# The modulation vectors of a hybrid diffusion block: products with w_mod on TensorE's four column groups in place of multiply-adds on VectorE, ScalarE and GpSimd

## The chip, the core and the metric

The kernel runs on one core of one Trainium2 chip. A core has five engines with a queue each: TensorE (PE in the profile, its weight loads PEld), VectorE (DVE), ScalarE (ACT), GpSimd (POOL) and SyncE (SP), which here issues all DMAs. The metric is the device time of one execution in microseconds (us).

## The reference, cut to what matters

Two layers (`DEPTH = 2`) run over 1024 latent tokens and 256 context tokens of width `D = 1024`. Ahead of each layer six modulation vectors are made for the latent stream (from `c`) and six for the context stream (from `c_ctx`): a product of a row of 1024 numbers with a 1024 x 6144 matrix, in float32.

```python
sc_x = jax.nn.silu(c)
sc_c = jax.nn.silu(c_ctx)
for l in range(DEPTH):
    with_ctx = l < DEPTH - 1
    mod_x = (sc_x @ w_mod[l] + b_mod[l])[:, None, :]
    mod_c = sc_c @ w_mod[l] + b_mod[l]
    sh1_x, s1_x, g1_x, sh2_x, s2_x, g2_x = jnp.split(mod_x, 6, -1)
    sh1_c, s1_c, g1_c, sh2_c, s2_c, g2_c = jnp.split(mod_c, 6, -1)
    hx = rmsnorm(x, g_pre_mix[l]) * (1 + s1_x) + sh1_x
    px = hx @ w_in[l]
    yx, yc = hybrid_mix(px, pc, ...)          # conv, retention, Fourier, neighbourhood attention
    x = x + g1_x * rmsnorm(yx @ w_out[l], g_post_mix[l])
    hx = rmsnorm(x, g_pre_ffn[l]) * (1 + s2_x) + sh2_x
    x = x + g2_x * rmsnorm(conv_ffn(hx, w_up[l], ffn_conv_w[l], w_down[l]), g_post_ffn[l])
    ...                                        # the same for ctx where with_ctx
```

## The kernel before

All large products run on TensorE as three float32r products each (high by high, high by low, low by high: lines 311 to 313, 335 to 337, 1069 to 1071, 1207 to 1209). The tokens lie in tiles of 128, eight of the latent stream and two of the context (numbers 8 and 9).

A layer runs in this order. `fnet` does the Fourier mixing (lines 409 to 455; in layer 0 also for the context, lines 436 to 448). `retention` goes over ten token tiles three times, with three sets of projected columns: values (evacuated by `ev_v`, line 498), keys (`ev_k`, with `rotate` at line 520 and products at line 542), and queries with gates (`ev_qg`, whose first ScalarE step is line 573). Neighbourhood attention, the convolution, the output projection and the gated MLP follow. In the MLP a group of two blocks of 128 hidden columns is projected up (`up`), and `down` takes it through eight token tiles, adding each result to `acc` on VectorE (line 1287).

The modulation is spread over this work by a Python generator. `mod_pool` does a little with each `next`. Layer 0 takes the first third of its columns (`t = 0`) from a routine of its own, `mod_front` (line 923, products of the 128 x 32 tile `sc` with 256 columns, in four column groups), ahead of all else; the other two thirds come from `it`, which advances by two at four places of each half of `fnet` and after each token tile of `retention` (`step(2)`). All of layer 1's modulation comes from `it2`, which advances in layer 0's MLP, once or twice after each tile of `down` (line 1288), and is run out in `ctx_h2` (line 1170). What is done at each step before: a 128 x 512 tile of `w_mod` has come by DMA, and it is multiplied by one column of `sc_c` and added to an accumulator, for the latent stream on VectorE (line 210), for the context in layer 0 by a product on ScalarE (line 207) and an addition on GpSimd (line 208). After eight such tiles `sums` adds the accumulator over partitions on TensorE, a float32 product of 512 columns with a 32-column tile of zeros and one column of ones (line 182), into the j-th 32 partitions of a PSUM bank `X`. After four of them the bank is copied (line 185), transposed (line 218), and added to the bias (line 224); for the gates two small DMAs of 4-byte elements write `grow` (line 246).

Each pool tag has a fixed number of buffers, and a DMA into one is issued once its last readers are done; SP issues in order, so what stands behind such a DMA waits too. The order of the instructions on each engine is set by a scheduler at build time, which keeps near the order of the program; TensorE and the other engines work their queues in order.

Of the kernel before, what the change touches and what calls it, by code (L numbers as in the profile page):

```python
# [8 lines left out]
AF = mybir.ActivationFunctionType  # L9
ALU = mybir.AluOpType  # L10
# [4 lines left out]
P = 128  # L15
# [5 lines left out]
KT = 8  # L21
# [7 lines left out]
def build(tc, d, out, dbg=None):  # L29
    nc = tc.nc  # L30
    act, dve, pool, pe, sp = nc.scalar, nc.vector, nc.gpsimd, nc.tensor, nc.sync
# [20 lines left out]
    cst = Pool("cst", bufs=1, side="left")  # L52
    lay = Pool("lay", bufs=2, side="left")
    hp_ = Pool("h", bufs=1, side="left")
# [26 lines left out]
    def X():  # L81
        return cur["pool"].t([P, 512], "X", cur["tags"]["X"])
# [10 lines left out]
    sc_c = cst.t([P, KT, 2], "sc_c")  # L93
    sp.dma_start(out=sc_c, in_=d["cc"])
    act.activation(sc_c, sc_c, AF.Silu)
    hot = cst.t([P, 33], "hot")
    dve.memset(hot, 0.0)
    dve.memset(hot[:, 1:2], 1.0)
    late = {}

    def late_consts():
# [53 lines left out]
        act.activation(m.cd, m.cd, AF.Exp)  # L155
        act.activation(m.cd, m.cd, AF.Exp, scale=-128.0)

    def mod_pool(m, ts, both, acc_tile, w_tile, ahead, tmp_tile=None):

        l = m.l
        work = [(t, j, k) for t in ts for j in range(4) for k in range(KT)]
        ws = {}

        def load(i):
            if i < len(work):
                t, j, k = work[i]
                w = ws[i] = w_tile(i)
                c0 = 2048 * t + 512 * j  # L170
                sp.dma_start(out=w, in_=d["w_mod"][l, P * k : P * k + P, c0 : c0 + 512])

        for i in range(ahead):
            load(i)
        later = []
        prs = {}

        def sums(t, j, acc, ns):
            if j == 0:
                prs[t] = X()  # L180
            for s in range(ns):
                pe.matmul(prs[t][32 * j : 32 * j + 32, :], hot[:, 1 - s : 33 - s], acc[:, s], start=(s == 0), stop=(s == ns - 1))
            if j == 3:
                mr = acc_tile()[:, 0]
                act.copy(mr, prs.pop(t))
                later.append((i + 2, lambda: mod_out(m, t, mr)))

        for i in range(len(work) + 8):
            if later and (i >= later[0][0] or i >= len(work)):
                later.pop(0)[1]()  # L190
            if i >= len(work):
                if not later:
                    return
                yield
                continue
            t, j, k = work[i]
            if k == 0:
                acc = acc_tile()
            load(i + ahead)
            w = ws.pop(i)  # L200
            ns = 1 + both(t)
            for s in range(ns):
                if k == 0:
                    act.activation(acc[:, s], w, AF.Copy, scale=sc_c[:, k, s : s + 1])
                elif s and tmp_tile:
                    p = tmp_tile()
                    act.activation(p, w, AF.Copy, scale=sc_c[:, k, s : s + 1])
                    pool.tensor_add(acc[:, s], acc[:, s], p)
                else:
                    dve.scalar_tensor_tensor(acc[:, s], w, sc_c[:, k, s : s + 1], acc[:, s], ALU.mult, ALU.add)  # L210
            if k == KT - 1:
                later.append((i + 8, lambda t=t, j=j, acc=acc, ns=ns: sums(t, j, acc, ns)))
            yield

    def mod_out(m, t, mr):
# [627 lines left out]
    m = mod_cols(0)  # L843
# [36 lines left out]
    for l in range(DEPTH):  # L880
        with_ctx = l < DEPTH - 1
        m = mods[l]
# [5 lines left out]
        if l == 0:  # L888
            xs = {t: (d["x"][P * t : P * t + P] if t < NT else d["ctx"][P * (t - NT) : P * (t - NT) + P]) for t in tiles}
            nm = Pool("nm0", bufs=1, side="left")  # L890
            hh, hl = h_tiles()
            ch, cl = hc_tiles()
            tok = Tok(hh, hl, ch, cl)
            sc = nm.t([P, KT, 32], "sc")
            dve.memset(sc, 0.0)
            dve.tensor_copy(sc[:, :, 0:2], sc_c)
            par1 = nm.t([P, KT], "par1")
            dve.tensor_scalar_add(par1, m.par[:, 8:16], 1.0)
            wm, xn = {}, {}

            def load_wm(k):
                if k < KT:
                    wm[k] = nm.t([P, KT, 256], "wm", 2)
                    sp.dma_start(out=wm[k], in_=d["w_modf"][k])

            def norm_in(t):
                x = xn[t] = nm.t([P, D], "xn", 10)
                sp.dma_start(out=x, in_=xs[t])
                ss = sm.t([P, 1], "ss")
                act.activation(raw_tile(), x, AF.Square, accum_out=ss)  # L910
                r = rstd_of(ss)
                dve.tensor_scalar_mul(x, x, r[:, 0:1])

            def mod_front(k):

                if k == KT:
                    return
                load_wm(k + 1)
                pr = X()
                w = wm.pop(k)  # L920
                for kk in range(KT):
                    j = kk % 4
                    pe.matmul(pr[32 * j : 32 * j + 32, 0:256], sc[:, kk, :], w[:, kk, :], start=(kk < 4), stop=(kk >= 4))
                mr = nm.t([P, 256], "mr", 2)
                act.copy(mr, pr[:, 0:256])
                for b in range(2):
                    pe.transpose(pr[:, 256 + P * b : 384 + P * b], mr[:, P * b : P * b + P], ident)
                red = sm.t([P, 2, 2], "red")
                dve.reduce_sum(red, pr[:, 256:512].rearrange("p (b j s) -> p b s j", b=2, j=4)[:, :, 0:2], axis=AX)
                dve.tensor_scalar(m.mc[:, 0, k], red[:, 0], m.par[:, k : k + 1], None, ALU.add)  # L930
                dve.tensor_scalar(m.a1[:, k], red[:, 1], par1[:, k : k + 1], m.par[:, 48 + k : 49 + k], ALU.add, ALU.mult)

            def lat_k(k):
                if k < KT:
                    for n0 in (0, 4):
                        ns = slice(P * n0, P * n0 + 512)
                        to_hk(k, [xn[t] for t in range(n0, n0 + 4)], hh[k][:, ns], hl[k][:, ns], m.a1, m.mc[:, 0], 0,
                              nm.t([P, 512], "tmp", 3), G())

            def ctx_k(k):  # L940
                to_hk(k, [xn[8], xn[9]], ch[:, k, :], cl[:, k, :], m.a1, m.mc[:, 0], 1, nm.t([P, 512], "tmp", 3), G())

            load_wm(0)
            for t in range(4):
                norm_in(t)
            ws = [weight(wi[0]), weight(wi[1])]
            for t in range(4, 8):
                norm_in(t)
            mod_front(0)
            lat_k(0)  # L950
            for t in (8, 9):
                norm_in(t)
            mod_front(1)
            late_consts()
            mod_small(m)
            pin = [M2(), M2()]
            for k in range(KT):
                lat_k(k + 1)
                if k + 2 <= KT:
                    mod_front(k + 2)  # L960
                for mm in range(2):
                    for ci, c in enumerate(LAT):
                        project(tok, ws[mm], c, pin[mm][:, 512 * ci : 512 * ci + 512], [k])
                ctx_k(k)
            nm.close()
        else:
            xs = nf.xs
            tok = Tok(nf.hh, nf.hl)
            ws = [weight(wi[0]), weight(wi[1])]
            pin = [M2(), M2()]  # L970
            for mm in range(2):
                for ci, c in enumerate(LAT):
                    project(tok, ws[mm], c, pin[mm][:, 512 * ci : 512 * ci + 512])
            tok.ch, tok.cl = nf.ctx([nf.load(t) for t in (8, 9)])
            nf.pool.close()


        if l == 0:
            it = mod_pool(m, (1, 2), lambda t: 1, lambda: mw.t([P, 2, 512], "ma", 2), lambda i: mw.t([P, 512], "mw", 4), 3,
                          lambda: mw.t([P, 512], "mp", 2))  # L980
        else:
            it = iter(())

# [6 lines left out]
        mw = Pool(f"mw{l}", bufs=1, side="right")  # L990
# [9 lines left out]
        kk = nat_k(tok, wi[13], kp, rest)  # L1000
# [8 lines left out]
        for hp in range(2):  # L1009
            if hp:  # L1010
                kk = nat_k(tok, wi[15], kp)
# [134 lines left out]
        if l + 1 < DEPTH:  # L1146
            m2 = mods[l + 1] = mod_cols(l + 1)
            mod_small(m2)

            mp = {}  # L1150

            def acc2():
                mp[0] = hp_.t([P, 4, 512], "HC", 2)
                return mp[0][:, 0:2]

            def w2(i):
                return mp[0][:, 2 + i % 2]

            it2 = mod_pool(m2, (0, 1, 2), lambda t: t == 0, acc2, w2, 0)
        else:  # L1160
            it2 = iter(())
        mxs = [0]
# [298 lines left out]
```

## Time and profile before

| | |
|---|---|
| time, median of 3 runs | 2867.41 us (2867.34 to 2869.33) |
| profiled execution: time | 2867.49 us |
| profiled execution: span of the trace | 2865.6 us |
| busy PE / PEld | 2763.4 us (96%) / 2277.0 us (79%) |
| busy DVE / ACT / POOL | 1634.7 us (57%) / 1079.2 us (38%) / 216.4 us (8%) |
| chain of work that ended last | PE 78%, DVE 4%, ACT 1%, DMA 1% |
| DMA | 271.30 MB, mean 95 GB/s |

The busy time of an engine is the time in which it runs an instruction; of TensorE the end of a product is modelled, and products overlap, so that two starts in a row tell what one costs and the length of one does not. The granted clock (PEclk) is the share of full speed that TensorE was given. The chain of work follows what released each instruction back from the end; a share of PE of 78% says that in most of the span TensorE waits for nobody.

### The profile page before, as it was taken

The numbers are of one execution on the slowest core, as the hardware profiler recorded it, in microseconds if no ns is written. First come the engines' busy times: TensorE is split into PE (matmuls) and PEld (weight loads), VectorE is DVE, ScalarE is ACT, GpSimd is POOL, SyncE is SP. The second block draws the span as 40 slices with busy tenths as digits, with TensorE's granted clock in tenths as the row PEclk, the third lists the DMA queues.
The fourth block names the chain that finished last, engine by engine and source line by source line (L and its number), as shares of the span: only waits on it lengthen the run. The fifth ranks groups of instructions, "written<-read, shape, count | busy, mean of one in ns | idle before, by whom it ended". The sixth has DMA issues, their size and how long they took to land.

```text
span 2865.6 us, 36418 instructions
## 1 busy us (share of the span) xinstructions
PE 2763.4 (96%) x14368; PEld 2277.0 (79%) x14368; DVE 1634.7 (57%) x2629; ACT 1079.2 (38%) x1785; POOL 216.4 (8%) x214
## 2 busy tenths in 40 slices
PE   7879999999999999989999999999999999999998
PEld 4767788887888788878779988788878888888886
DVE  5974464647456555555697855555553444444455
ACT  4542353535433333222356632354444322323331
POOL 0643100010000000000030000200000000000002
PEclk9989999999999999999999999999999999999999
DMA  6531312353222232242376531222521111111113
GB/s 247 195 103 33 79 39 69 108 168 119 66 74 81 74 103 81 70 107 74 87 259 220 176 101 30 62 62 64 179 95 43 57 47 52 46 51 52 44 46 124
DMA packets 142739, 271.30 MB, mean 95 GB/s; under 512 B 46948, under 2 KB 71015, under 8 KB 141543
## 3 DMA queue, kind: packets, MB, share of 16 engines
q1 hardware_dynamic: 142566, 268.96, 29.8%
q8 instruction: 113, 1.85, 0.3%
q14 instruction: 60, 0.48, 0.1%
HBM read 235.59 MB, written 28.34 MB: 92 GB/s over the span
## 4 chain that ended last, share of the span: by engine, by line
PE 78%; DVE 4%; ACT 1%; DMA 1%; issue 1%; POOL 1%; DVEq 0%; POOLq 0%; ACTq 0%; SPq 0%
PE G L312 15%; PE G L311 15%; PE G L313 15%; PE M L1207 6%; PE M L1208 5%; PE M L1209 5%; PE M L1071 2%; PE M L1070 2%; PE M L1069 2%; PE T L793 1%; PE G L335 1%; PE G L337 1%; PE G L336 1%; PE T L778 1%; DVE acc L1287 1%
## 5 line engine op out<-in xcount | busy, mean ns | idle before, releaser
L311 PE MATMUL G<-H,WH 128*128 128x512 f32 x1792 | 701.7, 392 | 9.6 <-DVE nkl L697 6.0
L312 PE MATMUL G<-H,WH 128*128 128x512 f32 x1792 | 700.4, 391 | 0.2
L313 PE MATMUL G<-H,WL 128*128 128x512 f32 x1792 | 700.2, 391 | 0.0
L117 DVE TENSOR_TENSOR WL<-RAW,WH 128x1024 fp32r<-128x1024 f32 x242 | 294.6, 1224 | 510.8 <-ACT WH L116 510.1
L116 ACT CAST WH<-RAW 128x1024 fp32r<-128x1024 f32 x242 | 252.3, 1051 | 587.7 <-PE G L312 379.9
L311 PEld LDWEIGHTS G<-H,WH 128*128 128x128 f32 x1792 | 336.6, 188 | 81.2 <-issue 12.3
L312 PEld LDWEIGHTS G<-H,WH 128*128 128x128 f32 x1792 | 336.5, 188 | 69.1 <-DVE H L274 1.2
L313 PEld LDWEIGHTS G<-H,WL 128*128 128x128 f32 x1792 | 336.5, 188 | 67.8 <-issue 0.5
L1207 PE MATMUL M<-WH,gh 128*128 128x512 f32 x744 | 296.2, 398 | 11.1 <-DVE acc L1287 10.4
L1208 PE MATMUL M<-WL,gh 128*128 128x512 f32 x744 | 294.2, 395 | 2.7 <-DVE WL L117 2.7
L1209 PE MATMUL M<-WH,gl 128*128 128x512 f32 x744 | 292.8, 394 | 0.0
L1287 DVE TENSOR_TENSOR acc<-M,acc 128x1024 f32<-128x1024 f32 x151 | 184.3, 1220 | 81.1 <-PE M L1209 79.4
L1207 PEld LDWEIGHTS M<-WH,gh 128*128 128x128 f32 x744 | 141.5, 190 | 48.7 <-DVE acc L1287 13.7
L1191 ACT COPY T<-G 128x512 f32<-128x512 f32 (+1 forms) x220 | 118.0, 536 | 154.0 <-PE G L313 144.7
L1208 PEld LDWEIGHTS M<-WL,gh 128*128 128x128 f32 x744 | 141.7, 190 | 32.0 <-DVE WL L117 3.6
L1209 PEld LDWEIGHTS M<-WH,gl 128*128 128x128 f32 x744 | 141.6, 190 | 30.8 <-DVE gl L1201 0.5
L345 DVE SCALAR_TENSOR_TENSOR T<-T,fcw,T 128x1023 f32<-128x1023 f32 (+1 forms) x132 | 134.0, 1015 | 35.9 <-ACT T L344 35.9
L313 PE MATMUL G<-HC,WL 128*128 128x256 f32 x496 | 140.5, 283 | 0.6 <-DVE WL L117 0.5
L312 PE MATMUL G<-HC,WH 128*128 128x256 f32 x496 | 141.0, 284 | 0.0
L311 PE MATMUL G<-HC,WH 128*128 128x256 f32 x496 | 140.6, 284 | 0.0
L335 PE MATMUL G<-WH,H 128*128 128x256 f32 (+1 forms) x384 | 129.2, 337 | 7.8 <-DVE rv L498 6.6
L346 DVE SCALAR_TENSOR_TENSOR T<-T,fcw,T 128x1023 f32<-128x1023 f32 (+1 forms) x132 | 134.1, 1016 | 3.8
(346 smaller groups left out, 4298.0 us busy)
## 6 DMA issues: line engine op xcount, KB each, us to landing
RAW<-in_w_up SPq DMA_DIRECT2D x132, 512.0 KB, 3.6
RAW<-in_w_down SPq DMA_DIRECT2D x66, 512.0 KB, 3.6
HC<-in_w_mod SPq DMA_DIRECT2D x96, 256.0 KB, 2.9
RAW<-in_w_in SPq DMA_DIRECT2D x44, 512.0 KB, 3.7
mw<-in_w_mod SPq DMA_DIRECT2D x64, 256.0 KB, 3.0
T<-xmid SPq DMA_DIRECT2D x20, 512.0 KB, 4.0
xmid<-x SPq DMA_DIRECT2D x18, 512.0 KB, 2.6
x<-xres SPq DMA_DIRECT2D x18, 512.0 KB, 4.5
```

Of the source, the lines that this page charges most:

```text
L116: act.copy(hi, raw)
L117: dve.tensor_sub(lo, raw, hi.bitcast(F32))
L311: pe.matmul(o, hi[:, wk], tok.cols(k, 0, c), start=(k == 0), stop=False)
L312: pe.matmul(o, hi[:, wk], tok.cols(k, 1, c), start=False, stop=False)
L313: pe.matmul(o, lo[:, wk], tok.cols(k, 0, c), start=False, stop=(k == KT - 1))
L335: pe.matmul(o, tok.cols(k, 0, c), hi[:, w], start=(k == 0), stop=False)
L345: dve.scalar_tensor_tensor(dst[:, a + 1 : b], src[:, a : b - 1], w[:, 0:1], dst[:, a + 1 : b], ALU.mult, ALU.add)
L346: dve.scalar_tensor_tensor(dst[:, a : b - 1], src[:, a + 1 : b], w[:, 2:3], dst[:, a : b - 1], ALU.mult, ALU.add)
L1207: pe.matmul(o, gh[:, tsl], hi[:, ns], start=start, stop=False)
L1208: pe.matmul(o, gh[:, tsl], lo[:, ns], start=False, stop=False)
L1209: pe.matmul(o, gl[:, tsl], hi[:, ns], start=False, stop=stop)
L1287: dve.tensor_add(acc[t], pt, acc[t])
```

## The change

`mod_pool` is written anew. The 128 x 32 tile `sc32`, two columns of which are the two streams' `silu` vectors for a block of 128 rows and the rest zero, stands from the start of the kernel, in place of `hot` and of `mod_front`'s `sc`. One unit of work is now a 128 x 2048 tile of `w_mod`, loaded by one DMA of 1 MB, and four float32 products of 512 columns each with `sc32[:, k]`, which go to the four column groups of one PSUM bank `X` and accumulate there over the eight `k`. The multiply-adds of lines 204 to 210, their accumulators and `sums` go. A unit takes four steps of the generator; the copy of the bank stands one step after the last unit's products, and `mod_out` (transposes, bias, gates) two steps behind that. A load is issued one unit ahead, into two buffers.

```diff
-    hot = cst.t([P, 33], "hot")
-    dve.memset(hot, 0.0)
-    dve.memset(hot[:, 1:2], 1.0)
+    sc32 = cst.t([P, KT, 32], "sc32")
+    dve.memset(sc32, 0.0)
+    dve.tensor_copy(sc32[:, :, 0:2], sc_c)
...
-    def mod_pool(m, ts, both, acc_tile, w_tile, ahead, tmp_tile=None):
+    def mod_pool(m, ts, w_tile, r_tile, ahead):
         l = m.l
-        work = [(t, j, k) for t in ts for j in range(4) for k in range(KT)]
+        work = [(t, k) for t in ts for k in range(KT)]
...
-                t, j, k = work[i]
-                w = ws[i] = w_tile(i)
-                c0 = 2048 * t + 512 * j
-                sp.dma_start(out=w, in_=d["w_mod"][l, P * k : P * k + P, c0 : c0 + 512])
+                t, k = work[i]
+                w = ws[i] = w_tile()
+                sp.dma_start(out=w, in_=d["w_mod"][l, P * k : P * k + P, 2048 * t : 2048 * t + 2048])
...
-            ns = 1 + both(t)
-            for s in range(ns):
-                if k == 0:
-                    act.activation(acc[:, s], w, AF.Copy, scale=sc_c[:, k, s : s + 1])
-                elif s and tmp_tile:
-                    p = tmp_tile()
-                    act.activation(p, w, AF.Copy, scale=sc_c[:, k, s : s + 1])
-                    pool.tensor_add(acc[:, s], acc[:, s], p)
-                else:
-                    dve.scalar_tensor_tensor(acc[:, s], w, sc_c[:, k, s : s + 1], acc[:, s], ALU.mult, ALU.add)
+            if k == 0:
+                pr = X()
+            for j in range(4):
+                pe.matmul(pr[32 * j : 32 * j + 32, :], sc32[:, k, :], w[:, 512 * j : 512 * j + 512], start=(k == 0), stop=(k == KT - 1))
+            yield
             if k == KT - 1:
-                later.append((i + 8, lambda t=t, j=j, acc=acc, ns=ns: sums(t, j, acc, ns)))
+                mr = r_tile()
+                act.copy(mr, pr)
+                yield
+                yield
+                mod_out(m, t, mr)
+            else:
+                yield
+                yield
             yield
...
-            it = mod_pool(m, (1, 2), lambda t: 1, lambda: mw.t([P, 2, 512], "ma", 2), lambda i: mw.t([P, 512], "mw", 4), 3,
-                          lambda: mw.t([P, 512], "mp", 2))
+            it = mod_pool(m, (1, 2), lambda: mw.t([P, 2048], "mw", 2), lambda: mw.t([P, 512], "ma", 1), 1)
...
-            it2 = mod_pool(m2, (0, 1, 2), lambda t: t == 0, acc2, w2, 0)
+            it2 = mod_pool(m2, (0, 1, 2), lambda: hp_.t([P, 2048], "HC", 2), lambda: hp_.t([P, 512], "HC", 2), 1)
```

Lines of the changed kernel are numbered anew: its line 182 is the new product, `fnet`'s lines 409, 421 and 436 are 389, 401 and 416 there, the products of `down` are 1174 to 1176, and `grow` is written at line 226. In the rows below, `M` and `X` are PSUM tiles, `HC`, `mw` and `RAW` SBUF tiles.

On TensorE, in the second half of layer 0's `fnet`, two sums stood before among the Fourier products:

```order
L335 MATMUL G<-WH,HC 128x256
L182 MATMUL X<-ma,hot 32x512
L421 MATMUL M_995<-tab,ab 128x257 x2
L424 MATMUL M_995<-ar,a_993 128x257
L421 MATMUL M_995<-tab,ab 128x256 x2
L421 MATMUL M_995<-tab,ab 128x255 x2
L182 MATMUL X<-ma,hot 32x512
L421 MATMUL M_995<-tab,ab 128x256 x2
```

Now four units, of four products each, stand in `fnet`; these are rows of its first half and of the start of its second, from the first unit to the third:

```order
L182 MATMUL X<-mw,sc_122 32x512 x4
L401 MATMUL M_885<-tab,ab 128x256 x2
L416 MATMUL M_918<-csg,ce 128x128
L417 MATMUL M_918<-csg,co 128x128
L418 MATMUL M_918<-csg,ce 1x128
L393 MATMUL M_950<-csg,z 1x128
L317 MATMUL G<-WH,HC 128x256
L182 MATMUL X<-mw,sc_122 32x512 x4
L424 MATMUL M_926<-tc_766,cab 128x128
L425 MATMUL M_926<-ar_764,c_924 128x128
```

A unit stands right in TensorE's queue, between products that need nothing of it, and its tile comes by a DMA that was issued one unit earlier.

On SP, in layer 0's MLP, the two DMAs that write layer 1's first gate rows stood before between loads of `w_mod` of 256 KB, eight of them right behind:

```order
L112 DMA RAW<-in_w_down 128x1024
L171 DMA HC<-in_w_mod 128x512 x3
L246 DMA grow_66<-gg 128x8x1 x2
L171 DMA HC<-in_w_mod 128x512 x8
L112 DMA RAW<-in_w_down 128x1024
```

Now they have one load of 1 MB ahead, that of the second unit after them, and two behind:

```order
L112 DMA RAW<-in_w_down 128x1024
L171 DMA HC<-in_w_mod 128x2048
L226 DMA grow_66<-gg 128x8x1 x2
L171 DMA HC<-in_w_mod 128x2048 x2
L112 DMA RAW<-in_w_down 128x1024
```

So the next two units' tiles, one loaded earlier and one by the load ahead, don't stand behind the gate rows.

## Rows read from the trace of the kernel before

**Rows 1.** The page's busy times: engine, us, share of the span, instructions.
```profile
PE 2763.4 (96%) x14368; PEld 2277.0 (79%) x14368; DVE 1634.7 (57%) x2629; ACT 1079.2 (38%) x1785; POOL 216.4 (8%) x214
```

**Rows 2.** Busy times by stretch: stretch, its length, engines' us (instructions), granted clock, DMA share, GB/s.
```profile
80.20:221.84 141.64, 115.97 (x741) 94.85 (x739) 119.19 (x201) 67.67 (x131) 81.17 (x53) 0.89 0.47 145
1675.20:1763.70 88.50, 88.28 (x680) 80.21 (x679) 50.58 (x161) 23.62 (x61) 2.32 (x2) 1.00 0.16 49
```

**Rows 3.** What PE waited for from 80 to 222 us: us in total, times, longest.
```profile
PE M L542 <- DVE rot L520: 14.1, 4, 6.7
PE G L335 <- DVE rv L498: 8.7, 4, 2.9
```

**Rows 4.** Groups of instructions from 80 to 222 us: count, busy, mean ns, idle before.
```profile
L208 POOL TENSOR_TENSOR ma<-ma,mp 128x512 f32<-128x512 f32 x53 | 81.4, 1537 | 104.0 <-ACT mp L207 69.1 <-ACT ma L204 31.6 <-DVE rv L498 0.5
L210 DVE SCALAR_TENSOR_TENSOR ma<-mw,sc_c,ma 128x512 f32<-128x512 f32 x49 | 58.1, 1186 | 9.2 <-DMA mw<-in_w_mod 6.7 <-ACT ma L204 2.0
L207 ACT ACTIVATE mp<-mw,sc_c 128x512 f32<-128x512 f32 x53 | 37.7, 721 | 45.1 <-DMA mw<-in_w_mod 26.2 <-POOL ma L208 18.7
...
L182 PE MATMUL X<-ma,hot 128*32 128x512 f32 x24 | 13.1, 668 | 2.6 <-DVE ma L210 2.6
```

**Rows 5.** PE's timeline, two visits of `sums` in the MLP: start us, us, instruction.
```profile
949.63 0.39 PE L1209 MATMUL M<-WH,gl 128*128 128x512 f32 x1
949.95 1.90 PE L182 MATMUL X<-HC,hot 128*32 128x512 f32 x4
951.79 0.50 PE L1207 MATMUL M<-WH,gh 128*128 128x512 f32 x1
952.13 0.40 PE L1208 MATMUL M<-WL,gh 128*128 128x512 f32 x1
...
1158.07 0.39 PE L1209 MATMUL M<-WH,gl 128*128 128x512 f32 x1
1158.39 1.05 PE L182 MATMUL X<-HC,hot 128*32 128x512 f32 x2
1159.37 0.50 PE L1207 MATMUL M<-WH,gh 128*128 128x512 f32 x1
1159.71 0.40 PE L1208 MATMUL M<-WL,gh 128*128 128x512 f32 x1
1159.94 0.39 PE L1209 MATMUL M<-WH,gl 128*128 128x512 f32 x1
```

**Rows 6.** PE's timeline, one visit of `mod_front`, eight products of 256 columns.
```profile
47.37 0.39 PE L311 MATMUL M<-H,WH 128*128 128x512 f32 x1
47.60 0.40 PE L312 MATMUL M<-H,WH 128*128 128x512 f32 x1
47.92 1.07 PE L923 MATMUL X<-wm,sc 128*32 128x256 f32 x16
48.92 0.50 PE L313 MATMUL M<-H,WL 128*128 128x512 f32 x1
49.27 0.49 PE L271 MATMUL G<-c_ident,xn 128*128 128x128 f32 x3
```

**Rows 7.** Busy times by stretch, as rows 2, in layer 0's MLP.
```profile
830.00:975.00 145.00, 145.00 (x626) 115.70 (x625) 91.22 (x91) 44.18 (x52) 0.00 (x0) 1.00 0.26 86
```

**Rows 8.** What PE waited for from 690 to 1365 us.
```profile
PE M L1207 <- DVE acc L1287: 7.6, 1, 7.6
```

**Rows 9.** The chain of waits around that wait: start us, us, what.
```profile
1230.32 11.95 DMA HC<-in_w_mod
...
1243.90 1.15 DVE acc L1287
...
1245.09 0.79 PE M L1207
1245.88 0.43 PE M L1208
```

**Rows 10.** DMA issues: engine, count, KB each, median us from issue to landing.
```profile
mw<-in_w_mod SPq DMA_DIRECT2D x64, 256.0 KB, 3.0
...
wm<-in_w_modf SPq DMA_DIRECT2D x8, 1024.0 KB, 5.1
...
grow<-gg SPq DMA_DIRECT2D x8, 4.0 KB, 10.7
```

More of the change, by code (lines that the diff above doesn't have):

```diff
@@ L167, in load @@
             if i < len(work):
-                t, j, k = work[i]
-                w = ws[i] = w_tile(i)
-                c0 = 2048 * t + 512 * j
-                sp.dma_start(out=w, in_=d["w_mod"][l, P * k : P * k + P, c0 : c0 + 512])
+                t, k = work[i]
+                w = ws[i] = w_tile()
+                sp.dma_start(out=w, in_=d["w_mod"][l, P * k : P * k + P, 2048 * t : 2048 * t + 2048])
         for i in range(ahead):
             load(i)
-        later = []
-        prs = {}
@@ L178, in sums @@
-        def sums(t, j, acc, ns):
-            if j == 0:
-                prs[t] = X()
-            for s in range(ns):
[L182 to L196, printed above, removed]
-            if k == 0:
-                acc = acc_tile()
+        pr = None
@@ L199, in mod_pool @@
+        for i, (t, k) in enumerate(work):
             load(i + ahead)
             w = ws.pop(i)
-            ns = 1 + both(t)
-            for s in range(ns):
-                if k == 0:
-                    act.activation(acc[:, s], w, AF.Copy, scale=sc_c[:, k, s : s + 1])
-                elif s and tmp_tile:
-                    p = tmp_tile()
-                    act.activation(p, w, AF.Copy, scale=sc_c[:, k, s : s + 1])
-                    pool.tensor_add(acc[:, s], acc[:, s], p)
-                else:
-                    dve.scalar_tensor_tensor(acc[:, s], w, sc_c[:, k, s : s + 1], acc[:, s], ALU.mult, ALU.add)
@@ L893, in build @@
             tok = Tok(hh, hl, ch, cl)
-            sc = nm.t([P, KT, 32], "sc")
-            dve.memset(sc, 0.0)
-            dve.tensor_copy(sc[:, :, 0:2], sc_c)
             par1 = nm.t([P, KT], "par1")
@@ L922, in mod_front @@
                     j = kk % 4
-                    pe.matmul(pr[32 * j : 32 * j + 32, 0:256], sc[:, kk, :], w[:, kk, :], start=(kk < 4), stop=(kk >= 4))
+                    pe.matmul(pr[32 * j : 32 * j + 32, 0:256], sc32[:, kk, :], w[:, kk, :], start=(kk < 4), stop=(kk >= 4))
                 mr = nm.t([P, 256], "mr", 2)
@@ L1148, in build @@
             mod_small(m2)
[L1150 to L1157, printed above, removed]
-            it2 = mod_pool(m2, (0, 1, 2), lambda t: t == 0, acc2, w2, 0)
+            it2 = mod_pool(m2, (0, 1, 2), lambda: hp_.t([P, 2048], "HC", 2), lambda: hp_.t([P, 512], "HC", 2), 1)
         else:
```

## Prediction

> **What bounds the kernel now.** I first read the page's busy times: TensorE (PE) is busy for 96% of the span [rows 1]. So the question is in which stretches it is not, and whether the modulation is why. Then the busy times by stretch, for the two places where the modulation runs.
>
> In layer 0 it runs beside the Fourier mixing and the first two passes of the retention. Layer 1 has the same code there without any modulation, since its own was made earlier, and this is the best witness in the trace. From the first Fourier product (line 409) to the first gate of the query pass (line 573) layer 0 takes 141.64 us and layer 1 88.50 us [rows 2]. In layer 1 PE is busy for 88.28 of them at a granted clock of 1.00; in layer 0 for 115.97, at a mean clock of 0.89, while VectorE is busy for 119.19, ScalarE for 67.67 and GpSimd for 81.17. The waits name the cause: PE waits 14.1 us for `rot` and 8.7 us for `rv`, both made on VectorE [rows 3], and what fills VectorE and GpSimd there are the multiply-adds [rows 4]. One such step takes VectorE 1186 ns and GpSimd 1537 ns.
>
> The accounts of layer 0 agree with the witness: of 141.64 us, 25.7 are idle PE, some 15.6 (0.11 of 141.64) lost clock, and about 12 the 24 records of `sums` [rows 4]; 88 are left, layer 1's figure.
>
> In layer 0's MLP, where layer 1's modulation is made, PE is busy all the time (145.00 of 145 us [rows 7]). There the multiply-adds lie beside PE and cost nothing, with one exception: a wait of 7.6 us [rows 8]. Its chain [rows 9] shows a load of `w_mod` that landed after 11.95 us, since the DMAs writing the gate rows stood ahead of it (they take 10.7 us [rows 10]); VectorE waited for it with `acc` queued behind, and PE for `acc`. After the wait a product took 0.43 us and not 0.23: the clock's lower level (1.2 in place of 2.4 GHz).
>
> **What a unit costs on TensorE.** A float32 product leaves two records. The MLP's timeline shows what products with a 32-column tile cost among others: there starts are about 0.227 us apart. A visit of one product takes 1.64 us from the start of the product before it to the start of the second one behind it, less two ordinary spacings 1.19; a visit of two, both in one column group, 2.50 less 0.45, that is 2.05 [rows 5]. So one float32 product of 512 columns takes 0.86, and about 0.33 is the price of coming and going.
>
> A unit is four products of 512 columns, one in each column group. Nothing in the trace has exactly this, but a visit of `mod_front` has the same columns in each group: eight products of 256, two per group. From 47.60 to 49.27 is 1.67 us, less 0.45 is **1.22 us** [rows 6]. One after another, eight such products at half of 0.86 would take 3.44 and the visit 3.77. The groups do run beside each other. The bounds for a unit are 1.19 below (one product alone) and 3.77 above (no overlap); I take 1.22, since that row differs in nothing but the width, and keep 1.1 to 1.4 for the range.
>
> The Trainium skill has another price. Its page "TensorE: Matmul & The Clock Gate", section "Measured speedup vs the span model", gives 3.07 times for four row tiles and 2.38 for three column tiles, less than the ideal. By 3.07 a unit would come to about 1.45 us by my estimate, and the sum below to about 9 us more; the trace disagrees, since its row shows the groups' overlap as nearly complete.
>
> **The sum.** Layer 0 has 16 units, layer 1's modulation 24.
>
> 1. *Layer 0, to the query pass.* The stretch of 141.64 us falls to layer 1's 88.50, plus 14 units (the steps put four in the Fourier mixing, five in each pass), plus waits w. 14 times 1.22 is 17.1. The change of PE's work is not hidden, since PE is then the bound. Before w: 88.5 + 17.1 - 141.6 = -36.0.
> 2. *The waits w.* PE now waits itself for a load, with everything behind it. A 1 MB load takes 5.1 us [rows 10], and with two buffers the load after next is issued only when a unit's products are done. In the retention a unit comes every two tiles, some 7 us; the load has more than that. In the Fourier mixing four units stand close, and the third and fourth loads, which SP also issues behind writes of its results, can be late: I put 4 us. Behind the first gate rows the 1 MB load of the third unit is late by perhaps 2 us. So w = 6; bounds 0 and 16 (four loads not hidden at all less the work between, and the gate rows' 10.7 half covered).
> 3. *Layer 0, query pass.* Two units more, 2.4 us; two visits of `sums` with two products each go, 4.1 us: -1.7. It runs at PE's pace, so nothing else changes.
> 4. *Layer 0's MLP.* 24 units add 29.3 us. `sums` goes: four visits of two products, 8.2, and eight of one, 9.5, in all 17.7. Net +11.6, all on the path. This is where the change costs time.
> 5. *The wait of 7.6 us*, and about 1.5 us of products at half pace after it, go: -9.1. The next unit's load was issued a unit earlier and the second one's is ahead of the gate rows in SP's order, so PE need not wait there. What is late next is the tile after those, which stands a whole up-projection away. The same gate DMAs at the end of the MLP still delay the context's loads; that stays.
>
> At nothing I cost: the memset and copy of `sc32` at the start (VectorE is idle there, waiting for loads); the bytes from HBM, which are the same; SP's 160 issues that become 40; the bank's copy and transposes, as many as before, beside `down`'s products; the relief of VectorE and ScalarE in the MLP, where PE waits for neither. If the copy were late, PE would stand for about a microsecond at each of five places; that is within w's range.
>
> Sum: -36.0 + 6 - 1.7 + 11.6 - 9.1 = **-29.2 us**. With u for a unit it is 40u + w - 84.0, so the change pays up to u = 1.95. The profiled execution took 2867.49 us, 0.08 above the median of the runs, so the forecast is **2838.3 us**, 1.0% faster.
>
> **Rivals.**
>
> *The wait moves to TensorE.* PE runs in order, and in layer 0 each late load stops all of it. If the four close units each wait a full 5.1 us, the gate rows block the queue for their 10.7 us, and the clock stays at its lower level after each wait as it did after the one in the MLP, w is about 33 (20.4, 10.7 and 2 for the clock) and the time 2865. For it: the load is only one unit ahead, where three small ones were before. Against: mean traffic before was 145 GB/s [rows 2], and the first loads land while PE is still at the first Fourier products.
>
> *It was the loads, not the engines.* If layer 0's stretch is held by the same bytes, it stays at 141.6 and only steps 3 to 5 count: +0.8, so 2868.3. Against it: PE's waits are for VectorE, and the multiply-adds there are idle for loads for 6.7 us only [rows 4].
>
> *The column groups don't overlap at this width.* A unit then costs 3.77 us, and 40 of them with w = 6 give +72.8: 2940.3, slower by 2.5%. It decides from 1.95 us a unit on. Against it stands the 256-column visit.
>
> *A smaller overlap.* If at 512 columns a quarter of one product's 0.86 us is lost in each unit, it costs 1.44 us, and the sum is -20.4: 2847.1. Against it stands the same visit, which loses less [rows 6]. The page of the Trainium skill named above has about such a factor.
>
> **How the numbers follow.** My case gets 0.76, the moved wait 0.12, the loads 0.04, no overlap 0.04, smaller overlap 0.04. My case's own range is u from 1.1 to 1.4 (-5 to +7) and w from 0 to 16 (-6 to +10): about 2827 to 2856, and the smaller overlap lies within it. I give 2826 to 2857, which leaves out about 0.2. Faster by over 0.2% (5.7 us; less can't be told from no change here) is my case, smaller overlap and part of the moved wait: 0.89. Within it the loads and some of the moved wait: 0.06. Slower: no overlap and a little of the moved wait: 0.05.
>
> **What would show it.** Right: the same stretch in layer 0 takes about 112 us with PE busy nearly throughout at a clock near 1.00, and the waits for `rot` and `rv` are mostly gone; a visit of a unit in the MLP reads 1.65 to 1.7 us between the starts around it, eight records; the MLP has no wait of 7 us, and PE is 100% busy in it with some 2.5 us more in all. Wrong: waits of PE for `mw` above 10 us in layer 0 (the first rival), PE idle as before with those waits gone (the second), or 3 us and more for a unit (the third).

## The result, and the profile after

The changed kernel takes 2830.93 us (median of 4 runs, 2829.87 to 2831.68) against 2867.38 us before (2866.67 to 2869.33): a ratio of 0.9872, 95% interval 0.9854 to 0.9889. That is 36.5 us less; the forecast was 29.2 less, and 2838.3 us in all. The span of the profiled execution is 2829.8 us, 35.8 below that of before.

In the code after the change the lines are renumbered: the new products are line 182, `down`'s are 1174 to 1176, its additions to `acc` 1254, the rotation 500, the bank's transposes 198.

The page's busy times (columns as rows 1):

```profile
PE 2761.1 (98%) x14624; PEld 2262.9 (80%) x14624; DVE 1483.0 (52%) x2459; ACT 1019.6 (36%) x1697; POOL 130.8 (5%) x158
```

Against [rows 1] VectorE lost 151.7 us, ScalarE 59.6 and GpSimd 85.6, while TensorE's busy time is the same within 2.3 us, in a span that is 35.8 us shorter. TensorE got no work taken off; it stands idle less and runs at full clock more.

The busy times by stretch of the changed kernel (columns as rows 2): the two stretches from the first Fourier product to the query pass, layer 0 and layer 1; then the first part and the rest of layer 0's query pass; then layer 0's MLP from its first up-projection (line 1158) to the first close of a tile (line 1213).

```profile
80.05:189.47 109.42, 109.42 (x829) 86.06 (x827) 48.87 (x159) 21.83 (x62) 0.00 (x0) 1.00 0.60 195
1639.40:1728.10 88.70, 88.48 (x681) 80.42 (x680) 50.60 (x161) 23.80 (x62) 2.32 (x2) 1.00 0.16 52
...
189.47:207.60 18.13, 17.75 (x102) 13.00 (x100) 4.37 (x13) 3.88 (x9) 2.36 (x3) 1.00 0.00 1
207.60:279.52 71.92, 69.11 (x427) 54.62 (x427) 37.17 (x91) 16.67 (x36) 21.60 (x25) 1.00 0.16 43
646.03:1397.94 751.91, 746.34 (x3382) 592.52 (x3382) 354.20 (x348) 239.03 (x290) 3.64 (x5) 1.00 0.27 84
```

The same three last stretches in the kernel before:

```profile
221.84:240.00 18.16, 15.06 (x68) 12.08 (x67) 10.16 (x21) 5.43 (x10) 5.40 (x5) 0.81 0.13 43
240.00:318.56 78.56, 75.36 (x452) 57.80 (x451) 39.05 (x94) 17.07 (x37) 23.52 (x28) 1.00 0.15 39
685.11:1435.46 750.35, 736.21 (x3222) 593.94 (x3222) 428.32 (x461) 250.32 (x306) 3.62 (x5) 0.99 0.28 85
```

Layer 0 to the query pass fell from 141.64 us [rows 2] to 109.4, and in it PE is busy for the whole of 109.42 at a clock of 1.00. The query pass fell from 96.72 us (18.16 and 78.56) to 90.05: before, its first 18 us had a clock of 0.81 and 68 records of products, now 102 in the same time. The MLP takes 1.6 us more.

What PE waited for from 60 to 340 us, which takes in the two thirds of layer 0's modulation that were changed:

```profile
PE M L556 <- DVE rot L500: 3.2, 8, 0.5
PE G L291 <- DVE cu L677: 1.8, 1, 1.8
PE G L291 <- DVE nkl L677: 1.4, 1, 1.4
```

The waits of [rows 3] (14.1 us for `rot`, 8.7 for `rv`) are gone, and no wait for `mw`, the tile of `w_mod`, took their place. The 8 waits for `rot` stand in the query pass, as 8 like them did before. From 640 to 1460 us, the MLP and its end, the first rows of the same view are:

```profile
PE M L1174 <- DVE acc L1254: 5.7, 2, 2.9
PE M L251 <- DVE T L245: 3.8, 1, 3.8
PE X L251 <- ACT t L252: 1.0, 1, 1.0
```

The wait of 7.6 us [rows 8] is gone. All of the longer ones come at the MLP's end: those of lines 251 and 252, 4.8 us, between 1300 and 1380 us, where layer 1's second gate rows are written, and the two for `acc` between 1400 and 1420, when tiles are closed and VectorE itself is busy with it. The kernel before had both kinds too (1365 to 1660 us, lines 271 and 272, together 6.2 us, and `acc`):

```profile
PE M L271 <- DVE T L265: 3.6, 1, 3.6
PE M L1207 <- DVE acc L1287: 2.9, 1, 2.9
...
PE X L271 <- ACT t L272: 2.6, 1, 2.6
```

A unit in the MLP, on PE's timeline (columns as rows 5):

```profile
719.92 0.39 PE L1176 MATMUL M<-WH,gl 128*128 128x512 f32 x1
720.24 1.06 PE L182 MATMUL X<-HC,sc 128*32 128x512 f32 x8
721.23 0.50 PE L1174 MATMUL M<-WH,gh 128*128 128x512 f32 x1
721.57 0.39 PE L1175 MATMUL M<-WL,gh 128*128 128x512 f32 x1
```

From 719.92 to 721.57 is 1.65 us, less two ordinary spacings (0.45) 1.20: eight records, four float32 products of 512 columns, for the price that the visit of 256 columns gave [rows 6]. The loads: `mw` 1 MB in a median of 5.4 us, the MLP's 5.0, and the gate rows 10.2, about as before [rows 10].

```profile
HC<-in_w_mod SPq DMA_DIRECT2D x24, 1024.0 KB, 5.0
...
mw<-in_w_mod SPq DMA_DIRECT2D x16, 1024.0 KB, 5.4
...
grow<-gg SPq DMA_DIRECT2D x8, 4.0 KB, 10.2
```

The account, from marks that both traces have (us from the span's start):

| to | before | after | gained in the stretch |
|---|---|---|---|
| first Fourier product, layer 0 | 80.20 | 80.17 | 0.0 |
| first gate of the query pass | 221.84 | 189.47 | 32.3 |
| end of the retention (last `yc`) | 318.56 | 279.52 | 6.7 |
| first up-projection of the MLP | 685.11 | 646.03 | 0.0 |
| first close of a tile | 1435.46 | 1397.94 | -1.6 |
| eighth close | 1467.37 | 1429.91 | -0.1 |
| end of the context's MLP | 1649.55 | 1613.92 | -1.8 |
| first Fourier product, layer 1 | 1675.20 | 1639.56 | 0.0 |
| end of the span | 2865.63 | 2829.81 | 0.2 |

### The profile page after: what moved, and what is told of

Read it like the earlier page. It is cut to its first block, busy times and chain, and to the rows that moved or that the text cites. A ratio compares the mean times of both kernels' runs of the same rounds, so it can differ in the third digit from the quotient of the medians.

```text
span 2829.8 us, 36199 instructions
## 1 busy us (share of the span) xinstructions
PE 2761.1 (98%) x14624; PEld 2262.9 (80%) x14624; DVE 1483.0 (52%) x2459; ACT 1019.6 (36%) x1697; POOL 130.8 (5%) x158
## 4 chain that ended last, share of the span: by engine, by line
PE 78%; DVE 4%; ACT 2%; DMA 2%; issue 1%; POOL 1%; POOLq 0%; DVEq 0%; SPq 0%; ACTq 0%
PE G L292 15%; PE G L291 15%; PE G L293 15%; PE M L1174 6%; PE M L1175 5%; PE M L1176 5%; PE M L1047 2%; PE M L1045 2%; PE M L1046 2%; PE T L773 1%; PE G L315 1%; PE G L317 1%; PE G L316 1%; PE X L182 1%; DMA RAW<-in_w_up 1%
## 5 line engine op out<-in xcount | busy, mean ns | idle before, releaser
L324 ACT ACTIVATE T<-T,fcw 128x1024 f32<-128x1024 f32 (+1 forms) x132 | 123.6, 936 | 12.5 <-DVE T L326 8.5
```

The costliest lines, as they stand in the source:

```text
L324: act.activation(dst[:, a:b], src[:, a:b], AF.Copy, scale=w[:, 1:2])
```

## The experiments

The theory: the gain is VectorE and GpSimd getting out of TensorE's way in layer 0, the MLP's part is about even, and four column groups run beside each other. Rivals: the gain is the fewer, larger loads; the MLP's wait for the gate rows is a part of it; or only the additions on GpSimd hurt, and the move to TensorE wasn't needed. Each run is compared with the kernel before on the same chip (median 2870.1, 2870.23 and 2869.69 us in the three sets; single executions from 2866.07 to 2872.64). Comparisons with the changed kernel go by the marks of one profiled execution each, so that a microsecond or two in them can be chance.

**Layer 0's part alone.** Layer 1's modulation in the MLP is done as before; `hot` lies in `sc32`'s place, which is free by then.

```diff
-            it2 = mod_pool(m2, (0, 1, 2), lambda: hp_.t([P, 2048], "HC", 2), lambda: hp_.t([P, 512], "HC", 2), 1)
+            it2 = mod_pool_old(m2, (0, 1, 2), lambda t: t == 0, acc2, w2, 0)
```

> The new products in layer 0 alone; in the MLP layer 1's modulation stays on VectorE and ScalarE as before. My theory: all of the gain is made in layer 0, where VectorE and GpSimd held PE up; the trace of the change is 39.1 us ahead when the retention ends. So 39 us off the kernel before, 2828 us (2826 to 2831), at or a little below the whole change, with the wait of 7.6 us in the MLP still there. Rival: the MLP's part pays as well (its wait goes), then this alone is slower than the whole change, 2835 us or more.

2833.93 us, ratio 0.9872 (0.9855 to 0.9888); span 2831.0. The time lies above the expected range, the ratio is that of the whole change. It is 38.8 us ahead of before at the retention's end and gives 4 of them back: its MLP still has the wait behind the gate rows and one at its end, where the kernel before had 6.2 us:

```profile
PE M L1243 <- DVE acc L1323: 8.3, 1, 8.3
PE X L308 <- ACT t L309: 7.7, 2, 7.5
```

The whole gain is in layer 0.

**The MLP's part alone.**

```diff
-            it = mod_pool(m, (1, 2), lambda: mw.t([P, 2048], "mw", 2), lambda: mw.t([P, 512], "ma", 1), 1)
+            it = mod_pool_old(m, (1, 2), lambda t: 1, lambda: mw.t([P, 2, 512], "ma", 2), lambda i: mw.t([P, 512], "mw", 4), 3,
+                          lambda: mw.t([P, 512], "mp", 2))
```

> The new products in the MLP alone; layer 0's modulation stays on the three engines. My theory: 24 units of 1.2 us less the old sums' 17.7 us cost 11 us on PE, the wait that goes gives back 9: 2.5 us slower than before by these terms, 3.4 by the two traces, so 2869 to 2872 us. Rival: the relief of VectorE and ScalarE pays there, below 2863 us.

2872.27 us, ratio 1.0010 (1.0000 to 1.0019), just above the expected range; span 2870.5. Its waits from 690 to 1445 us begin:

```profile
PE X L308 <- ACT t L309: 6.7, 1, 6.7
PE M L1236 <- DVE acc L1316: 2.9, 1, 2.9
```

The 7.6 us for `acc` are gone; the 2.9 stand at 1442 us, where a tile is closed, and the kernel before has them there too. The 6.7 stand where it waited 6.2. But 24 units cost more than the `sums` that they replace: to the first close of a tile the MLP takes 3.3 us more than before. Where PE is always busy, the change costs a few us or nothing that can be told.

**All four products in one column group.** Each unit's four products go to the same 32 partitions, so that none can run beside another; the bank is cleared first. Three quarters of the modulation's columns are left out of the result and the rest is a sum of all four.

```diff
-                pe.matmul(pr[32 * j : 32 * j + 32, :], sc32[:, k, :], w[:, 512 * j : 512 * j + 512], start=(k == 0), stop=(k == KT - 1))
+                pe.matmul(pr[0:32, :], sc32[:, k, :], w[:, 512 * j : 512 * j + 512], start=(k == 0 and j == 0), stop=(k == KT - 1 and j == 3))
```

> All four products of a unit go to the first column group, one after another, after the bank was set to zero on VectorE; three quarters of the modulation of these columns are left out and the rest is mixed up. My theory: the four groups run beside each other, a unit of 1.2 us becomes one of 3.7 to 3.8, and 40 units add about 100 us to the whole change's time: 2925 to 2940 us. Rival: the groups were hardly overlapped, or PE has room beside its products, and the time stays within 20 us of the whole change.

One execution: 2924.87 us, span 2923.0, 93.2 above the changed kernel's, or 2.33 us a unit (39.9 over 16 units in layer 0, 55.5 over 24 in the MLP; 2.1 come back behind it). A unit on its timeline:

```profile
750.40 0.39 PE L1177 MATMUL M<-WH,gl 128*128 128x512 f32 x1
750.71 3.62 PE L183 MATMUL X<-HC,sc 128*32 128x512 f32 x8
754.26 0.50 PE L1175 MATMUL M<-WH,gh 128*128 128x512 f32 x1
754.60 0.40 PE L1176 MATMUL M<-WL,gh 128*128 128x512 f32 x1
```

From 750.40 to 754.60 is 4.20, less 0.45 it is 3.75, where the prediction's bound without overlap was 3.77. So the groups' overlap is what makes the change pay: without it the kernel would be slower than before by 2%. Less the 0.33 us of coming and going, four products take 0.87 us in four groups and 3.42 in one: 3.9 times. The Trainium skill, page "TensorE: Matmul & The Clock Gate", section "Measured speedup vs the span model", gives 2.38 for three column tiles and 3.07 for four row tiles; here the loss is smaller than that.

**Before, without the context's multiply-adds in layer 0.** The kernel before; layer 0's `t` = 1 and 2 are made for the latent stream alone, so that the products on ScalarE and the additions on GpSimd for the context are left out (and the context's result is not the reference's). Loads and VectorE's multiply-adds stay.

```diff
-            it = mod_pool(m, (1, 2), lambda t: 1, lambda: mw.t([P, 2, 512], "ma", 2), lambda i: mw.t([P, 512], "mw", 4), 3,
+            it = mod_pool(m, (1, 2), lambda t: 0, lambda: mw.t([P, 2, 512], "ma", 2), lambda i: mw.t([P, 512], "mw", 4), 3,
```

> The kernel before, with the context's modulation of layer 0 left out for two thirds of its columns (its multiply-adds on ScalarE and GpSimd, and half of the sums, go; VectorE's 56 steps stay). First theory: GpSimd's additions slow VectorE's steps down (1186 ns beside them, 746 in the MLP, where GpSimd is idle), so without them VectorE's steps fall to about 750 ns, the stretch of 141.6 us falls to 100 to 110, and the time to 2828 to 2838 us. Second theory: it is the number of VectorE's steps that holds PE, whatever GpSimd does; then VectorE's steps stay near 1.1 us and only the sums go, 7 us, 2855 to 2862 us.

2832.93 us, ratio 0.9866 (0.9851 to 0.9881): as much as the whole gain, with the 64 loads of 256 KB and VectorE's work as before. VectorE's group from 80 to 200 us (columns as rows 4):

```profile
L210 DVE SCALAR_TENSOR_TENSOR ma<-mw,sc_c,ma 128x512 f32<-128x512 f32 x56 | 41.6, 743 | 17.2 <-DMA mw<-in_w_mod 16.0 <-ACT ma L204 0.8
```

The busy times of the stretch to the query pass, which begins at 192 us:

```profile
80.00:192.00 112.00, 101.68 (x729) 86.32 (x727) 81.14 (x211) 27.47 (x71) 0.00 (x0) 0.95 0.60 185
```

The same instruction took a mean of 1186 ns in the kernel before [rows 4] and takes 743 here. VectorE's busy time in the stretch is 81.14 us against 119.19, although it does as many multiply-adds, and the stretch is 112 us against 141.64. The run leaves out ScalarE's products and GpSimd's additions together; which of them slowed VectorE is to be read in the kernel before. Its timeline of VectorE and GpSimd:

```profile
129.01 0.74 DVE L210 SCALAR_TENSOR_TENSOR ma<-mw,sc_c,ma 128x512 f32<-128x512 f32 x1
130.34 0.73 DVE L210 SCALAR_TENSOR_TENSOR ma<-mw,sc_c,ma 128x512 f32<-128x512 f32 x1
131.31 8.48 POOL L208 TENSOR_TENSOR ma<-ma,mp 128x512 f32<-128x512 f32 x5 [4.85 <-ACT mp L207]
132.00 3.15 DVE L210 SCALAR_TENSOR_TENSOR ma<-mw,sc_c,ma 128x512 f32<-128x512 f32 x2
```

Of the 49 multiply-adds [rows 4], 12 had no addition of GpSimd's beside them and took 731 to 754 ns, whether or not ScalarE was busy; the 25 that lay beside one for over nine tenths of their time took 1475 in the mean. So it is GpSimd's additions.

The stretch is not free of waits here. PE is busy for 101.68 of 112 us, and its longest wait is a load's:

```profile
PE M L542 <- DVE rot L520: 8.1, 1, 8.1
...
160.68 0.75 DVE L210 SCALAR_TENSOR_TENSOR ma<-mw,sc_c,ma 128x512 f32<-128x512 f32 x1 [8.46 <-DMA mw<-in_w_mod]
```

This multiply-add waited for a tile of `w_mod` that came behind layer 0's first gate rows, and `rot` stood in VectorE's queue behind it. The longest wait for `rot` in the kernel before, 6.7 us [rows 3], came about in the same way:

```profile
179.75 0.75 DVE L210 SCALAR_TENSOR_TENSOR ma<-mw,sc_c,ma 128x512 f32<-128x512 f32 x1 [6.75 <-DMA mw<-in_w_mod]
```

So the loads' number and size are not what held layer 0 in the main (that rival falls), but a part of the waits was a late load, and the changed kernel, whose tile behind the same gate rows lands 12.5 us after its issue, does not wait for it. The main cause was the second stream, which cost VectorE through GpSimd. On TensorE that second stream is one more column of a 32-column tile. Whether VectorE could have taken both streams itself was not run: 53 more steps at 743 ns are 39 us, and on top of its 81 they would fill more than the 112 us, by an estimate from these rows.

**One buffer for `mw` in layer 0**, with no load ahead.

```diff
-            it = mod_pool(m, (1, 2), lambda: mw.t([P, 2048], "mw", 2), lambda: mw.t([P, 512], "ma", 1), 1)
+            it = mod_pool(m, (1, 2), lambda: mw.t([P, 2048], "mw", 1), lambda: mw.t([P, 512], "ma", 1), 0)
```

> The whole change, with one buffer for layer 0's tiles of w_mod in place of two, each loaded only when the unit before is done. My theory: a 1 MB load takes 5.4 us; in the retention a unit comes every 7 us or later, so the loads still hide there; in the Fourier mixing four units stand 4 to 6 us apart, and each waits 2 to 5 us: 8 to 15 us in all on the whole change, 2839 to 2846 us. Rival of the prediction (PE pays for the loads): every one of 16 units waits, 60 us and more, above 2885 us.

One execution: 2846.09 us, span 2844.3, 14.5 above the changed kernel's. Of these, 2.9 come ahead of the first Fourier product, where the first 1 MB load is issued at 53 us, ahead of loads of `w_in`, and not at 76 behind them. From 80 to 112 us, in the Fourier mixing, PE waits for no load; from 112 to 170:

```profile
PE X L182 <- DMA mw<-in_w_mod: 9.1, 3, 4.8
```

The total came out as expected, the place didn't: the waits are in the retention's passes, the longest for a load that stood behind the first gate rows, and not where four units stand close. This is the wait of the first rival, and the second buffer hides all of it.

**Layer 1's gate rows later.** The two pairs of DMAs that write layer 1's `grow` stand at the start of its retention, not in layer 0's MLP.

```diff
-            gate_rows(m, 0)
+            gates.append((m, 0)) if m.l else gate_rows(m, 0)
...
         rp = Pool(f"rp{l}", bufs=1, side="left")
+        while gates:
+            mm, which = gates.pop(0)
+            gc = rp.t([P, KT, 2], f"gc{which}", 1)
+            dve.tensor_copy(gc, mm.gg[:, which])
+            for s in range(2):
+                sp.dma_start(out=grow[mm.l][which, s].rearrange("(k p) -> p k", p=P), in_=gc[:, :, s])
```

> The whole change, with layer 1's gate rows written to memory in layer 1, after its Fourier mixing, not in layer 0's MLP. My theory: the context's loads at the end of the MLP stand no longer behind them, so that PE's waits there, 3.8 and 1.0 us with their clock loss, shrink: 3 to 8 us off the whole change, 2823 to 2828 us. Rival: something else holds these loads, and the time stays at 2831.

2837.35 us, ratio 0.9887 (0.9872 to 0.9901), span 2833.4, slower than expected: it is 9.0 us ahead of the changed kernel at layer 1's first Fourier product, and then gives 12.5 back by the query pass. From 1620 to 1760 us, PE's waits, and the load that the chain of waits leads back to:

```profile
PE G L317 <- DVE rv L480: 10.9, 2, 10.8
...
1655.88 15.77 DMA rw<-in_rmat
```

That load stood right behind the four DMAs, and VectorE's work on it ahead of `rv`. In the kernel before, too, the load behind such DMAs took 11.95 us [rows 9]; the question is whether anyone needs that load at once.

**Layer 1's modulation on VectorE, without GpSimd.** Layer 0 as in the change. In the MLP VectorE makes multiply-adds of 1024 columns, ScalarE the first of each eight, and the accumulators are summed for a third of the columns at a time in the four column groups (the third with both streams in two halves): four visits of PE in place of 24.

```diff
+            for s in range(2 if t == 0 else 1):
+                h = s if t == 0 else p
+                a = acc[:, 1024 * h : 1024 * h + 1024]
+                if k == 0:
+                    act.activation(a, w, AF.Copy, scale=sc_c[:, k, s : s + 1])
+                else:
+                    dve.scalar_tensor_tensor(a, w, sc_c[:, k, s : s + 1], a, ALU.mult, ALU.add)
...
+                    for j in range(4):
+                        pe.matmul(pr[32 * j : 32 * j + 32, :], hot[:, 1:33], acc[:, 512 * j : 512 * j + 512], start=True, stop=True)
...
-            it2 = mod_pool(m2, (0, 1, 2), lambda: hp_.t([P, 2048], "HC", 2), lambda: hp_.t([P, 512], "HC", 2), 1)
+            it2 = mod_vec(m2, hot)
```

> Layer 0 as in the change; layer 1's modulation in the MLP by multiply-adds of 1024 columns on VectorE, with the sums over partitions of a whole third at once in the column groups: four visits of PE in place of 24. My theory: VectorE has room beside PE there and PE has none, so 28.8 us of units become 6.5: 22 us off the whole change, 2806 to 2813 us. Rival: VectorE's longer steps stand ahead of the additions to acc, PE waits for them, and half or more is given back: 2820 us or more.

2809.78 us, ratio 0.9790 (0.9776 to 0.9805), 22.6 us ahead of the changed kernel at the first close of a tile: in this stage TensorE is the bound, and VectorE has room (busy for 419.7 of 729.5 us). The longest wait left is 5.3 us, behind a load of 9.9 us that the gate rows delay. From 640 to 1450 us:

```profile
PE M L1230 <- DVE acc L1310: 9.3, 3, 5.3
```

**Both of these together.**

> The last two together. If they are independent, both gains add up: 25 to 30 us off the whole change, 2800 to 2807 us. If the late gate rows give nothing, the same as the version with VectorE in the MLP.

2814.51 us, ratio 0.9817 (0.9800 to 0.9833): 8.5 us ahead of the run without the late gates at layer 1's start, 4.0 behind it at the end; it gave the gain back in the value pass, as the run with the late gate rows alone did. The expected sum of both gains did not come; moving the gate rows to there isn't worth anything.

**Gate rows in layer 1's query pass.** The same two pairs of DMAs, at two tiles of layer 1's query pass, where no load that is needed soon stands close behind.

```diff
         def ev_qg(t, o):
+            if l and t in (1, 3):
+                mm, which = gates.pop(0)
+                gc = rp.t([P, 256], "rot", 2)[:, 0:16].rearrange("p (k s) -> p k s", s=2)
```

> The whole change, with layer 1's gate rows written in the query pass of layer 1's retention, where no weights are to come for some 60 us; the version before wrote them ahead of the value pass, where PE then waited 10.8 us. My theory: the 9 us that it was ahead at layer 1's Fourier mixing are kept, 2820 to 2824 us. Rival: these DMAs hold something up wherever they stand, 2829 us or more.

2824.14 us, ratio 0.9841 (0.9827 to 0.9856), at the upper end of what was expected; span 2820.7: the span is 9.1 us below the changed kernel's, and nothing is given back. From 1300 to 1760 us, where the waits at the MLP's end and the value pass's 10.8 us both would stand, two of the rows are:

```profile
PE M L1182 <- DVE acc L1262: 2.9, 1, 2.9
...
PE M L564 <- DVE rot L502: 1.5, 4, 0.4
```

**Both of the parts that paid**: the multiply-adds in the MLP and the gate rows in the query pass.

> The version with layer 1's modulation on VectorE, and the gate rows in the query pass of layer 1. My theory: both gains add up, 8 to 10 us off the 2809.8 us of that version, 2799 to 2803 us, some 28 to 32 us below the whole change. Rival: as for the run before, 2808 us or more.

2802.99 us, ratio 0.9768 (0.9752 to 0.9785), span 2801.8: the fastest of the study, 28 us below the change by the spans, and 67 below the kernel before on the same chip. From 640 to 1450 us PE waits no longer than 2.9 us at once:

```profile
PE M L1238 <- DVE acc L1318: 5.7, 2, 2.9
```

## Why the prediction was right, and where its sizes were off

It was right in sign and in the main mechanism, and its time was 7.4 us too long; by the spans the gain was 6.6 us more than the sum.

*What bounds.* Right: idle TensorE in layer 0, behind VectorE and GpSimd. That it was in the main the engines and not the loads is shown by the run without the context's multiply-adds, which has the old loads and as much gain. The prediction's ground against the loads, 6.7 us without one, was weaker than it looked: PE's longest wait for `rot`, also 6.7, followed from just that. It did not see that VectorE's 1186 ns were a result of GpSimd's additions; its sum didn't need it.

*A unit, 1.22 us.* Measured 1.20, and 3.75 in one column group where the bound was 3.77. "No overlap" falls. "A smaller overlap" would have shown a unit of 1.44 us; it falls too, and with it the price by the Trainium skill's page, 1.45.

*Steps 1 and 2.* Forecast -36.0 + 6 for the stretch and what follows it, 111.6 us for the stretch with all of w in it; measured 109.4, a gain of 32.3. Both terms were off, in opposite ways. PE waits for no load, so w was 0. But layer 1, the witness, has no Fourier mixing for the context, and layer 0 does: the 32 records of lines 416 to 428 lie in the stretch and were not in its 88.50. 88.5 + 17.1 is 105.6, and 3.8 are missing to 109.4, in which PE is always busy. By the starts around them (88.88 to 89.63, 91.25 to 92.93, 101.61 to 102.56 and 103.39 to 104.97 us) these records take about 5.0: they fill the gap, and 1.2 us that the stretch is shorter are not accounted for. The prediction's account of the 141.64 us, which came out at layer 1's figure, left no room for them either: some of its other terms were too large. "The wait moves" falls in this kernel; the run with one buffer shows it at 9.1 us and that the second buffer is what keeps it away.

*Step 3, the query pass: the step that failed.* Forecast -1.7 ("it runs at PE's pace, so nothing else changes"), measured -6.7. It did not run at PE's pace at its start. The row of before shows its first 18.16 us at a clock of 0.81, and what PE waited for from 221 to 241 us there was

```profile
PE M L576 <- ACT rot L510: 3.1, 1, 3.1
```

and on ScalarE the copy that makes this `rot` stood behind a product for the context, which had waited for GpSimd (and the products ahead of it for a late load):

```profile
229.82 0.72 ACT L207 ACTIVATE mp<-mw,sc_c 128x512 f32<-128x512 f32 x1 [1.22 <-POOL ma L208]
230.45 0.35 ACT L510 COPY rot<-G 128x256 f32<-128x256 f32 x1
```

The products behind the wait start 0.43 us apart and not 0.23, up to 236 us:

```profile
234.49 0.63 PE L335 MATMUL G<-WH,H 128*128 128x512 f32 x1
234.92 0.63 PE L336 MATMUL G<-WL,H 128*128 128x512 f32 x1
```

So the multiply-adds ran on into the pass, and the idle time and the lower level of the clock did not stop at the first gate, where the prediction had closed its stretch. The 3.1 us of the wait and about 2 of the slower products make up the 5 us between -1.7 and -6.7, most of the miss of 7.

*Step 4 and 5, the MLP.* Forecast +11.6 and -9.1, in all +2.5; measured +1.6 to the first close. Most of the difference lies at the MLP's end, where the prediction changed nothing and PE waited 6.2 us before and some 5 now. The run with the MLP's part alone agrees: +3.3 us to the first close, +2.2 in all by the medians. What was named as staying, the delay by the gate rows at the MLP's end, stays: 4.8 us of waits at lines 251 and 252 between 1300 and 1380 us, none of which is left in the run with the gate rows in the query pass.

*Left open.* From the eighth close to the end of the context's MLP the changed kernel takes 184.01 us and the kernel before 182.18. PE's busy time is the same within 0.3 us, so the 1.8 us are mostly idle, and 1.1 of them are waits for `gh`, which ScalarE makes (1.5 against 0.4 us). Why ScalarE is later there is not shown: between the first close and layer 1's first Fourier product layer 0's part alone loses 1.8 us, with no instruction of the change there, the MLP's part alone 2.2, the run with VectorE in the MLP 2.5, and the one with the gate rows in the query pass nothing.

## What to carry to other kernels

A stretch that a side job slows does not end where the job's stage ends: look for its tail, in idle time and in the granted clock, in the stage behind. A float32 product with few columns of weights costs TensorE little when it comes four at a time into four column groups, and a second row of inputs costs nothing more; but it pays only where TensorE was waiting, and where it is the bound already, the same work belongs on an engine with room, as the run with VectorE in the MLP shows by 22.6 us. A DMA of many 4-byte elements belongs where no load that is needed soon stands behind it in its queue; moving it only from one such place to another gains nothing.

## What the runs showed of the hardware that was not expected

- A multiply-add of 128x512 float32 on VectorE took a mean of 1186 ns in a stretch in which GpSimd made additions on tiles of that size, and 743 ns when those were left out: 1.6 times, at the same place in the program. In the kernel before itself it took 731 to 754 ns with no addition beside it and 1475 in the mean beside one. VectorE's own busy time hides this; it looked like VectorE's price.
- Four float32 products of 512 columns in four column groups took 1.20 us with coming and going, 0.01 more than the 1.19 of a single one [rows 5].
- DMAs of 1024 four-byte elements, issued in pairs and 10.2 us long in the median, delayed the loads behind them by about as much. With two pairs ahead of layer 1's value pass a load took 15.77 us and PE waited 10.8; taking them out of layer 0's MLP brought 9.0 us; in the query pass they cost nothing that shows.
